# A hybrid encoder layer on one core: GpSimd's readers of SBUF go to VectorE or ScalarE, and the planner's dense matmul gets another cost

## The chip, the cores and the metric

The kernel runs on one core of a Trainium2 chip. The core has five engines with a queue of instructions each: TensorE (PE, matmuls from SBUF into PSUM), VectorE (DVE), ScalarE (ACT), GpSimd (POOL) and SyncE (SP), which here issues nearly all transfers. Each engine works through its queue in order, and an instruction waits until the results that it reads are there. The metric is the time of one execution in microseconds (us), as the median of several runs.

## The reference

One layer of a streaming encoder is applied to 2048 prompt frames and 32 frames of a running stream, 2080 columns in all, 1024 features wide, in float32. After an RMS norm, one input projection feeds three groups of mixers that read the frames in time order: an RG-LRU (256 features), an RWKV-7 (6 heads of 64, a state of 64 x 64 a head) and an mLSTM (6 heads of 64). Their outputs go through one output projection; a SwiGLU network with 2816 hidden units follows, and a last RMS norm.

```python
hn = rmsnorm(x, norm1)
proj = hn @ w_in                                    # 1024 x 3072
ya = rmsnorm(rg_lru(...), norm_a) * gelu(pa_g)      # columns one after another
yb = rwkv7_mix(...); yc = mlstm_mix(...)
x = x + concat([ya, yb, yc]) @ w_out                # 1024 x 1024
gu = rmsnorm(x, norm2) @ w_ffn_in                   # 1024 x 5632
x = x + (silu(gu[:, :2816]) * gu[:, 2816:]) @ w_ffn_out
y = rmsnorm(x, norm_f)                              # and all new states
```

## The kernel before

**Stages.** The columns are cut into four parts: three of 512 and one of 544 (512 prompt and 32 sample columns, worked as two blocks of 272). Every projection holds features on the partitions and columns along the free dimension. `innorm` and `inproj` do the norm and the input projection of a part, 24 row tiles of 128 outputs, and write them to a scratch in DRAM (`spill`). `mixers` reads that back in pieces of 128 columns, 16 for the prompt and a last one of 32 sample columns: 17 groups of an RWKV, an mLSTM and an RG-LRU part each, which write `ymix` in DRAM. `phase2` does output projection, SwiGLU and the sums for a part; it needs that part's `ymix`. All four input projections come first, then mixers and `phase2` of each part in turn.

**Dense matmuls.** A projection is made of three float32r products: every weight block and every activation is split into a leading part and the exact rest (`split`: ScalarE copies the leading part, another engine subtracts). `mm3` adds leading x leading, leading x rest and rest x leading into one PSUM tile `pj`. In the names `wh`/`wl` are the two parts of a weight block of 128x1024, `hh`/`hl` those of hidden units, or of a weight block in the hidden units' place, `ah`/`al` those of the normed input. In `inproj`, GpSimd makes the weights' rests (`load_w(..., G, True)`); elsewhere VectorE does.

**A group of the RWKV.** Decays and removal keys are normed (`k<-k,k` are Newton steps of the key norm's inverse root, 128x6), the bonus is summed by a product with `bones` (its operand split into `ch` and `cl`), and products `rw<-Fr,BK` give the chunk's interaction matrices `Hr`. Their 32-blocks are inverted row by row on VectorE (`utmp` and `Z`, 62 instructions in line, after and before a trip through DRAM). `rw<-ta,Hr` and `rw<-c,En` complete the inverse; then come the state products (`SV`, `zc`, `UV`, `Un`), the head norm (`yx`) and the write to `ymix`.

**Who sets the order.** Nothing is emitted while the program is written down. A `Recorder` notes each instruction with its operands and a level of urgency (`EVAC`, `WGT`, `NORM`, `MIX`, `PROJ`, `LATE`); `Recorder.order` then fills the engines' queues by list scheduling: the engine that can start first takes its most urgent instruction that is ready, by the durations that `cost` states. So a cost changes no instruction, only places in the queues. On TensorE the mixers' products have a share: each adds its planned time to `debt`, each projection matmul takes `RATE` = 0.45 of its own planned time off, and mixers are held back while `debt` is too high or too few are ready.

```python
if eng == "dve":
    if name in ("tensor_copy", "tensor_scalar") and ins[0].space != PSUM:
        return 68.0 + 0.53 * n, 127.0
...
    return 68.0 + 1.04 * n + (61.0 if ptr and n > 1 and len(ins) > 1 else 0.0), 127.0
...
return 125.0 + (2.15 if name == "tensor_tensor" else 1.0) * n, 127.0      # GpSimd
```

All instructions are emitted from one line (L332 of the profile), so the profile tells them apart by their tiles.

Of the kernel before, what the change touches and what calls it, by code (L numbers as in the profile page):

```python
# [11 lines left out]
F32 = mybir.dt.float32  # L12
F32R = mybir.dt.float32r
I32 = mybir.dt.int32
AF = mybir.ActivationFunctionType
# [12 lines left out]
# columns of the per-feature vectors, 128 features a column  # L28
# [13 lines left out]
# columns of the constants  # L42
# [11 lines left out]
# columns of the small weights  # L54
# [41 lines left out]
class Cfg:  # L96
    def __init__(self, seq, sb1, sb2):
        # sb1: list of (prompt tokens, column blocks); the 32 sample tokens follow the last prompt token
        # sb2: list of (first column, column blocks)
        self.seq = seq  # L100
        self.T = seq + 32
        self.sb1 = sb1
        self.sb2 = sb2
# [10 lines left out]
# PE's share for the mixers, relative to the projections, and how long they may hold it at a time (ns)  # L114
RATE = 0.45
BURST = 1200.0
# allowance for the mixers' operands (ns)
# [13 lines left out]
# transfers issued ahead of the one under way (ns)  # L131
WINDOW = 3000.0
# the projection's tile before which the next columns are normed
NEXT = 14
# urgency, on the other engines and on PE; the lowest goes first
# [12 lines left out]
class Recorder:  # L148
    """Stands in for the engines: notes each instruction with its operands, so that the order of issue
    can be chosen before the instructions are emitted (under tc.manual_schedule, which keeps it)."""  # L150
# [93 lines left out]
    def order(self):  # L244
        """greedy: the engine that can start first takes its most urgent instruction that is ready"""
# [102 lines left out]
def cost(eng, name, out, ins, kw):  # L348
    """nanoseconds on the engine, and until another engine sees the result"""
# [8 lines left out]
    if eng == "pe":  # L358
# [3 lines left out]
        if st.dtype == F32R:  # L362
            return max(n, 256) / 2.4 + 2.7, 196.0
# [26 lines left out]
class Tiles:  # L390
    """fixed tiles, taken in turn: name -> bufs tiles"""
# [30 lines left out]
def hybrid_kernel(ctx, tc, A, O, cfg):  # L422
# [48 lines left out]
    def rsqrt_(x, y, t, it=3):  # L471
        """y = 1/sqrt(x), Newton from the exponent halved"""
# [7 lines left out]
    def log1p_(e, out2, tmp):  # L480
        """out2 = log(1+e)/2 for 0 <= e <= 1, by the series of atanh(e/(2+e)); tmp: two tiles"""
# [10 lines left out]
    # the gates' weights, row selections; histories and running states: stream 0 the prompt, 1 the sample  # L492
# [11 lines left out]
    def setup():  # L504
# [9 lines left out]
        # derived vectors  # L514
# [8 lines left out]
        # -4 softplus(-lam)  # L523
# [1114 lines left out]
```

## Time and profile before

| | |
|---|---|
| runs | 2943.65, 2947.76 and 2950.33 us, median 2947.76 us |
| span of the profiled execution, first to last instruction | 2943.6 us (its whole time is not given) |
| instructions | 48657 |
| mean granted clock of TensorE | 0.979 of full speed |
| dense matmuls | 7056 of 512 columns, 4704 of 272 |
| HBM | 268.51 MB read, 46.27 MB written, 107 GB/s over the span |

The page lists for each engine the time in which it was busy. That is an average over stretches that differ: at first input projections and mixers run together, then `phase2` of the first three parts with the mixers, and in the last part `phase2` alone. A table by stretches keeps them apart. The granted clock is a mean over a stretch: 1.00 is 2.4 GHz, and 0.5 would be 1.2 GHz throughout. Names are the program's tiles, output first (`wl<-raw,wh`), buffer numbers left out; sizes are partitions x elements.

### The profile page before, as it was taken

The numbers are of one execution on the slowest core, as the hardware profiler recorded it, in microseconds if no ns is written. First come the engines' busy times: TensorE is split into PE (matmuls) and PEld (weight loads), VectorE is DVE, ScalarE is ACT, GpSimd is POOL, SyncE is SP. The second block draws the span as 40 slices with busy tenths as digits, with TensorE's granted clock in tenths as the row PEclk, the third lists the DMA queues.
The fourth block names the chain that finished last, engine by engine and source line by source line (L and its number), as shares of the span: only waits on it lengthen the run. The fifth ranks groups of instructions, "written<-read, shape, count | busy, mean of one in ns | idle before, by whom it ended". The sixth has DMA issues, their size and how long they took to land.

```text
span 2943.6 us, 48657 instructions
## 1 busy us (share of the span) xinstructions
PE 2797.9 (95%) x17643; PEld 2301.3 (78%) x17643; DVE 2190.3 (74%) x5580; ACT 1217.7 (41%) x2555; POOL 704.9 (24%) x839
## 2 busy tenths in 40 slices
PE   7989889989999999999999999999999999999998
PEld 6767667778877777777777777777777778999998
DVE  6776887777778877888888887888666776555555
ACT  4444454444454434445544444363433334322223
POOL 5644344344312011112311011122011112211102
PEclk9999999999999999999999999999999999999999
DMA  6353334253433233324433323334332334232222
GB/s 210 112 160 109 123 123 128 100 165 100 122 100 98 82 104 99 91 72 128 139 111 92 96 87 101 93 107 138 93 107 82 93 87 162 74 90 87 87 90 81
DMA packets 235212, 317.95 MB, mean 108 GB/s; under 512 B 63100, under 2 KB 146988, under 8 KB 234844
## 3 DMA queue, kind: packets, MB, share of 16 engines
q1 hardware_dynamic: 233820, 313.74, 35.0%
q8 instruction: 138, 2.26, 0.3%
q10 hardware_dynamic: 1152, 1.11, 0.1%
q14 instruction: 102, 0.84, 0.1%
HBM read 268.51 MB, written 46.27 MB: 107 GB/s over the span
## 4 chain that ended last, share of the span: by engine, by line
PE 61%; DVE 20%; DMA 5%; issue 2%; ACT 2%; POOL 1%; SPq 0%; DVEq 0%; ACTq 0%; POOLq 0%
PE pj L332 51%; PE rw L332 7%; DVE wl L332 4%; PE ml L332 3%; DMA xs<-tb 3%; DVE utmp L332 1%; DVE Z L332 1%; DVE stg L332 1%; DVE x L332 1%; DVE k L332 1%; DMA tb<-Hr 1%; DVE Fr L332 1%; DVE R L332 1%; DVE al L332 1%; DVE Dm L332 1%
## 5 line engine op out<-in xcount | busy, mean ns | idle before, releaser
L332 PE MATMUL pj<-ah,wh 128*128 128x512 f32 (+1 forms) x2560 | 905.8, 361 | 4.1 <-ACT cbuf L332 1.8
L332 PE MATMUL pj<-al,wh 128*128 128x512 f32 (+1 forms) x2560 | 903.8, 360 | 4.4 <-DVE al L332 4.4
L332 PE MATMUL pj<-ah,wl 128*128 128x512 f32 (+1 forms) x2560 | 836.4, 358 | 2.0 <-DVE wl L332 2.0
L332 ACT ACTIVATE wh<-raw 128x1024 fp32r<-128x1024 f32 (+2 forms) x444 | 382.2, 862 | 759.2 <-PE pj L332 587.5
L332 PEld LDWEIGHTS pj<-ah,wh 128*128 128x128 f32 x2560 | 488.6, 191 | 73.1 <-issue 2.7
L332 PEld LDWEIGHTS pj<-al,wh 128*128 128x128 f32 x2560 | 490.7, 192 | 69.2 <-DVE al L332 6.0
L332 PEld LDWEIGHTS pj<-ah,wl 128*128 128x128 f32 x2560 | 458.8, 191 | 71.4 <-DVE wl L332 3.0
L332 DVE TENSOR_TENSOR wl<-raw,wh 128x1024 fp32r<-128x1024 f32 (+2 forms) x397 | 412.6, 1041 | 61.7 <-ACT wh L332 58.7
L332 POOL TENSOR_TENSOR stg<-stg,rb 128x512 f32<-128x512 f32 (+1 forms) x110 | 155.2, 1419 | 893.8 <-DVE stg L332 771.0
L332 PE MATMUL pj<-hl,wh 128*128 128x512 f32 (+1 forms) x856 | 302.2, 360 | 2.7 <-DVE hl L332 2.1
L332 PE MATMUL pj<-hh,wh 128*128 128x512 f32 (+1 forms) x856 | 299.7, 361 | 3.5 <-ACT hh L332 3.5
L332 PE MATMUL pj<-hh,wl 128*128 128x512 f32 (+1 forms) x856 | 279.5, 356 | 0.0
L332 DVE TENSOR_TENSOR x<-x,pj 128x512 f32<-128x512 f32 (+1 forms) x280 | 159.1, 583 | 134.9 <-PE pj L332 133.2
L332 PEld LDWEIGHTS pj<-hl,wh 128*128 128x128 f32 x856 | 161.6, 189 | 28.3 <-DVE hl L332 7.0
L332 PEld LDWEIGHTS pj<-hh,wh 128*128 128x128 f32 x856 | 160.1, 188 | 28.8 <-ACT hh L332 6.7
L332 PE MATMUL pj<-ah,hh 128*128 128x512 f32 (+1 forms) x480 | 173.1, 367 | 7.3 <-ACT hh L332 5.8
L332 PE MATMUL pj<-al,hh 128*128 128x512 f32 (+1 forms) x480 | 174.7, 370 | 2.5 <-DVE al L332 2.5
L332 DVE TENSOR_TENSOR utmp<-Z,xs 96x60 f32<-96x60 f32 (+27 forms) x527 | 135.7, 258 | 51.1 <-DMA xs<-tb 36.4
L332 PEld LDWEIGHTS pj<-hh,wl 128*128 128x128 f32 x856 | 152.3, 188 | 22.3
L332 POOL TENSOR_TENSOR wl<-raw,wh 128x1024 fp32r<-128x1024 f32 x47 | 114.8, 2444 | 191.1 <-ACT wh L332 186.9
L332 PE MATMUL pj<-ah,hl 128*128 128x512 f32 (+1 forms) x480 | 160.1, 365 | 0.0
L332 POOL TENSOR_TENSOR hl<-raw,hh 128x512 fp32r<-128x512 f32 x92 | 126.7, 1379 | 114.6 <-ACT hh L332 106.1
(348 smaller groups left out, 4222.1 us busy)
## 6 DMA issues: line engine op xcount, KB each, us to landing
raw<-in_w_ffn_in SPq DMA_DIRECT2D x176, 512.0 KB
raw<-in_w_ffn_out SPq DMA_DIRECT2D x128, 256.0 KB
raw<-in_w_in SPq DMA_DIRECT2D x96, 256.0 KB
raw<-in_w_in SPq DMA_DIRECT2D x48, 512.0 KB
spill<-stg SPq DMA_DIRECT2D x72, 256.0 KB
raw<-in_w_out SPq DMA_DIRECT2D x32, 512.0 KB
x<-in_xT SPq DMA_DIRECT2D x48, 256.0 KB
raw<-in_w_ffn_out SPq DMA_DIRECT2D x64, 192.0 KB
```

What stands on the lines that cost most here:

```text
L332: o.fn(*o.args, **o.kw)
```

## The change

Every GpSimd instruction that reads SBUF goes to another engine: two-operand arithmetic and the scalings to VectorE, copies to ScalarE. GpSimd keeps memsets. In the planner the matmul with float32r operands costs n / 2.25 + 4.0 ns instead of n / 2.4 + 2.7. Comments and docstrings are removed as well, which touches no instruction.

```diff
 # the planner's cost of a matmul with float32r operands (n: columns): ns on the engine, ns to the reader
-            return max(n, 256) / 2.4 + 2.7, 196.0
+            return max(n, 256) / 2.25 + 4.0, 196.0
 # innorm, square(k)
-                G.tensor_tensor(out=acc, in0=acc, in1=sq, op=ALU.add)
+                V.tensor_tensor(out=acc, in0=acc, in1=sq, op=ALU.add)
 # inproj, conv()
-                G.tensor_copy(buf[:, 0:3], hist[st])
-                G.tensor_copy(hist[st], buf[:, m:m + 3])
+                S.activation(buf[:, 0:3], hist[st], AF.Copy)
+                S.activation(hist[st], buf[:, m:m + 3], AF.Copy)
 # inproj
-            w = first_w.pop(0) if first_w else load_w(w_in(m), 8, G, True)
+            w = first_w.pop(0) if first_w else load_w(w_in(m), 8, V, True)
-                        G.tensor_copy(tm[:, 0:1], histmu[st][:, m:m + 1])
-                        G.tensor_copy(histmu[st][:, m:m + 1], tm[:, q:q + 1])
+                        S.activation(tm[:, 0:1], histmu[st][:, m:m + 1], AF.Copy)
+                        S.activation(histmu[st][:, m:m + 1], tm[:, q:q + 1], AF.Copy)
 # rglru: four instructions, G to V
-            G.tensor_scalar(out=la[:, m, :], in0=tr[:, m, :], scalar1=1.0, scalar2=D("nsp", i=m),
+            V.tensor_scalar(out=la[:, m, :], in0=tr[:, m, :], scalar1=1.0, scalar2=D("nsp", i=m),
...
-        G.tensor_tensor(out=q, in0=q, in1=gb, op=ALU.mult)
+        V.tensor_tensor(out=q, in0=q, in1=gb, op=ALU.mult)
 # rwkv
-        G.tensor_tensor(out=cl_, in0=cf, in1=ch_.bitcast(F32), op=ALU.subtract)
+        V.tensor_tensor(out=cl_, in0=cf, in1=ch_.bitcast(F32), op=ALU.subtract)
-            G.tensor_copy(UV[oh, :, :nch, j, :], SVt[oh, :, :nch, j, :])
+            S.activation(UV[oh, :, :nch, j, :], SVt[oh, :, :nch, j, :], AF.Copy)
-                G.tensor_copy(UN[c][hs, :, j, :], UV[hs, :, c, j, :])
+                S.activation(UN[c][hs, :, j, :], UV[hs, :, c, j, :], AF.Copy)
 # phase2
-                G.tensor_tensor(out=acc[:, o:o + N], in0=acc[:, o:o + N], in1=sq, op=ALU.add)
+                V.tensor_tensor(out=acc[:, o:o + N], in0=acc[:, o:o + N], in1=sq, op=ALU.add)
-                    G.tensor_tensor(out=u, in0=u, in1=rb2[:, o:o + N], op=ALU.mult)
+                    V.tensor_tensor(out=u, in0=u, in1=rb2[:, o:o + N], op=ALU.mult)
-                        (G if last and k % 3 == 2 else V).tensor_tensor(out=y, in0=y, in1=rb, op=ALU.mult)
+                        V.tensor_tensor(out=y, in0=y, in1=rb, op=ALU.mult)
```

The order of issue follows from the new engines and the new cost. VectorE's queue, in the first group's key norm (`k_0_230`, `k_0_233` and `k_0_236` are its three small tiles; `ca`, `stg` and `sq<-pj` belong to the input projection, `BK` and `c` to the group), read before:

```order
L332 TENSOR_SCALAR k_0_233<-k_0_230 128x6
L332 SCALAR_TENSOR_TENSOR stg_202<-stg_202,ca_206 128x512
L332 TENSOR_TENSOR sq_180<-pj_199,acc_126 128x512
L332 TENSOR_TENSOR k_0_236<-k_0_233 128x6
L332 TENSOR_TENSOR BK_240<-sq_228,En_226 64x6x64
L332 SCALAR_TENSOR_TENSOR k_0_236<-k_0_236,k_0_230 128x6
L332 TENSOR_TENSOR BK_240<-sq_228,En_226 64x6x64
L332 SCALAR_TENSOR_TENSOR k_0_233<-k_0_236,k_0_233 128x6
L332 TENSOR_TENSOR k_0_236<-k_0_233 128x6
L332 SCALAR_TENSOR_TENSOR k_0_236<-k_0_236,k_0_230 128x6
L332 SCALAR_TENSOR_TENSOR k_0_233<-k_0_236,k_0_233 128x6
```

and in the changed kernel:

```order
L332 TENSOR_SCALAR k_0_233<-k_0_230 128x6
L332 TENSOR_TENSOR BK_240<-sq_228,En_226 64x6x64
L332 SCALAR_TENSOR_TENSOR stg_202<-stg_202,ca_206 128x512
L332 TENSOR_TENSOR sq_180<-pj_199,acc_126 128x512
L332 TENSOR_TENSOR wl_144<-raw_141,wh_142 128x1024
L332 TENSOR_TENSOR k_0_236<-k_0_233 128x6
L332 TENSOR_TENSOR c_168<-c_168,sq_228 128x384
L332 SCALAR_TENSOR_TENSOR k_0_236<-k_0_236,k_0_230 128x6
L332 SCALAR_TENSOR_TENSOR ca_206<-cbuf_205,vec_76,ca_206 128x512
L332 TENSOR_TENSOR hl_0_147<-raw_140,hh_0_146 128x512
L332 SCALAR_TENSOR_TENSOR ca_206<-cbuf_205,vec_76,ca_206 128x512
L332 TENSOR_TENSOR acc_127<-acc_127,sq_180 128x512
```

The weights' rests (`wl`, `hl`) and the row sums (`acc`) of the next columns now stand between the steps of the key norm.

TensorE's queue at the last RWKV group, where its inverse is completed and its state used (`pj` are dense matmuls, here of the third `phase2`, `rw` the group's), read before:

```order
L332 MATMUL pj_201<-al_0_171,wh_142 128x512
L332 MATMUL rw_165<-ta_167,Hr_125 32x32 x6
L332 MATMUL pj_201<-ah_0_170,wl_144 128x512
L332 MATMUL pj_201<-ah_0_172,wh_142 128x512
L332 MATMUL pj_201<-al_0_173,wh_142 128x512
L332 MATMUL pj_201<-ah_0_172,wl_144 128x512
L332 MATMUL rw_166<-c_168,En_226 32x32 x6
L332 MATMUL rw_165<-SV_150,Fr_124 64x64 x4
L332 MATMUL pj_201<-ah_0_174,wh_142 128x512
L332 MATMUL pj_201<-al_0_175,wh_142 128x512
```

and in the changed kernel, where the dense matmuls are already those of the last `phase2` (272 columns):

```order
L332 MATMUL pj_200<-ah_0_172,wh_143 128x272
L332 MATMUL pj_200<-al_0_173,wh_143 128x272
L332 MATMUL pj_200<-ah_0_172,wl_145 128x272
L332 MATMUL rw_165<-ta_167,Hr_125 32x32 x6
L332 MATMUL rw_166<-c_168,En_226 32x32 x3
L332 MATMUL rw_165<-SV_150,Fr_124 64x64
L332 MATMUL rw_166<-c_168,En_226 32x32 x3
L332 MATMUL rw_165<-SV_150,Fr_124 64x64 x3
L332 MATMUL rw_166<-zc_229,c_168 64x64 x6
L332 MATMUL rw_165<-UV_247,Fr_124 64x64 x6
L332 MATMUL rw_166<-Un_0_120,Hr_125 64x128
```

The group's products follow each other now with no dense matmul between them; before, dense matmuls stood between most of the steps.

## Rows read from the trace of the kernel before

**Rows 1.** page, part 1: busy us (share of the span) xinstructions

```profile
PE 2797.9 (95%) x17643; PEld 2301.3 (78%) x17643; DVE 2190.3 (74%) x5580; ACT 1217.7 (41%) x2555; POOL 704.9 (24%) x839
```

**Rows 2.** busy by stretch: stretch, us, five engines, TensorE's clock, DMA share, GB/s

```profile
0.00:120.30 120.30, 98.86 (x432) 76.94 (x432) 78.75 (x126) 55.46 (x99) 70.08 (x85) 0.98 0.53 177
120.30:846.50 726.20, 662.48 (x4462) 544.09 (x4463) 554.45 (x1527) 335.83 (x775) 298.65 (x389) 0.96 0.40 124
846.50:2430.30 1583.80, 1543.60 (x8959) 1198.50 (x8957) 1280.88 (x3416) 660.85 (x1395) 245.58 (x287) 0.99 0.34 100
2484.00:2943.60 459.60, 443.20 (x3493) 440.20 (x3491) 239.19 (x442) 138.59 (x238) 77.44 (x69) 0.98 0.30 90
```

**Rows 3.** TensorE's waits, 120.3 to 846.5: us in total, times, longest

```profile
PE rw L332 <- ACT ch L332: 9.9, 3, 6.1
PE ml L332 <- DVE gt L332: 8.1, 2, 5.4
```

**Rows 4.** chain that ended last, in order of time: start, us, what

```profile
2035.35 40.85 PE pj L332 x175
2796.82 125.52 PE pj L332 x997
```

**Rows 5.** timeline at 109 to 121: start, us, engine, line, operation, [idle before]

```profile
109.31 2.40 POOL L332 TENSOR_TENSOR wl<-raw,wh 128x1024 fp32r<-128x1024 f32 x1 [2.24 <-ACT wh L332]
109.52 2.21 DVE L332 TENSOR_TENSOR k<-k 128x6 f32<-128x6 f32 x1
120.31 0.69 PE L332 MATMUL rw<-ch,bones 128*128 128x384 f32 x1 [6.13 <-ACT ch L332]
```

**Rows 6.** VectorE's groups by shape: xcount | busy us, mean ns | idle before

```profile
L332 DVE TENSOR_TENSOR wl<-raw,wh 128x1024 fp32r<-128x1024 f32 x209 | 289.2, 1384 | 21.9 <-ACT wh L332 20.8
L332 DVE TENSOR_TENSOR x<-x,pj 128x512 f32<-128x512 f32 x168 | 114.2, 683 | 60.1 <-PE pj L332 58.5 <-DMA x<-in_xT 0.2
L332 DVE TENSOR_TENSOR x<-x,pj 128x272 f32<-128x272 f32 x112 | 44.9, 434 | 74.9 <-PE pj L332 74.7
L332 DVE TENSOR_TENSOR hl<-stg,hh 128x272 fp32r<-128x272 f32 x44 | 30.5, 694 | 4.8 <-ACT hh L332 4.8
L332 DVE SCALAR_TENSOR_TENSOR k<-k,k 128x6 f32<-128x6 f32 x96 | 34.7, 361 | 0.9
```

**Rows 7.** VectorE's instructions of two tiles: xcount: ns min/median/max

```profile
L332 DVE SCALAR_TENSOR_TENSOR k<-k,k x102: 145/166/2190, 112.1 to 2366.0; 128x6 f32<-128x6 f32 x96, 64x6 f32<-64x6 f32 x6
L332 DVE TENSOR_TENSOR utmp<-Z,xs x527: 135/209/2457, 159.0 to 2421.9; 96x60 f32<-96x60 f32 x16, 96x28 f32<-96x28 f32 x12, 96x66 f32<-96x66 f32 x11, 96x48 f32<-96x48 f32 x10
```

**Rows 8.** page, part 5: a group, xcount | busy us, mean ns | idle before

```profile
L332 DVE TENSOR_TENSOR utmp<-Z,xs 96x60 f32<-96x60 f32 (+27 forms) x527 | 135.7, 258 | 51.1 <-DMA xs<-tb 36.4
```

**Rows 9.** GpSimd's groups by shape

```profile
L332 POOL TENSOR_TENSOR wl<-raw,wh 128x1024 fp32r<-128x1024 f32 x47 | 114.8, 2444 | 191.1 <-ACT wh L332 186.9 <-PE ml L332 4.1
L332 POOL TENSOR_TENSOR hl<-raw,hh 128x512 fp32r<-128x512 f32 x92 | 126.7, 1379 | 114.6 <-ACT hh L332 106.1 <-PE rw L332 2.6 <-ACT En L332 2.3
L332 POOL TENSOR_TENSOR stg<-stg,rb 128x512 f32<-128x512 f32 x66 | 105.1, 1593 | 558.3 <-DVE stg L332 435.5 <-DVE utmp L332 69.7 <-DVE Z L332 46.5
L332 POOL TENSOR_TENSOR stg<-stg,rb 128x272 f32<-128x272 f32 x44 | 50.0, 1157 | 335.6 <-DVE stg L332 335.6
L332 POOL TENSOR_TENSOR acc<-acc,cbuf 128x512 f32<-128x512 f32 x42 | 70.6, 1680 | 117.3 <-ACT cbuf L332 117.0
L332 POOL TENSOR_TENSOR acc<-acc,sq 128x512 f32<-128x512 f32 x21 | 31.4, 1497 | 12.7 <-ACT ah L332 6.3 <-DVE sq L332 5.4 <-ACT sq L332 0.4
```

**Rows 10.** ScalarE's copy of 64x192, by shape

```profile
L332 ACT ACTIVATE SV<-rw 64x192 f32<-64x192 f32 x66 | 21.4, 325 | 12.5 <-PE rw L332 11.6
```

**Rows 11.** timeline at the last RWKV group's end

```profile
2430.30 0.38 PE L332 MATMUL rw<-ta,Hr 32*32 32x32 f32 x12
2452.41 0.40 PE L332 MATMUL rw<-cst,yx 64*128 64x64 f32 x3
2466.45 1.75 DVE L332 TENSOR_TENSOR al<-sq,ah 128x544 fp32r<-128x544 f32 x2 [0.60 <-ACT ah L332]
```

More of the change, by code (lines that the diff above doesn't have):

```diff
@@ L855, in rglru @@
         S.activation(s2, h, AF.Square)
-        G.tensor_tensor(out=s2[:, 0, :], in0=s2[:, 0, :], in1=s2[:, 1, :], op=ALU.add)
+        V.tensor_tensor(out=s2[:, 0, :], in0=s2[:, 0, :], in1=s2[:, 1, :], op=ALU.add)
         rb = la[:, 0, :]
@@ L863, in rglru @@
         S.activation(q, gb, AF.Square)
-        G.tensor_scalar(out=q, in0=q, scalar1=0.044715, scalar2=1.0, op0=ALU.mult, op1=ALU.add)
-        G.tensor_tensor(out=q, in0=q, in1=gb, op=ALU.mult)
+        V.tensor_scalar(out=q, in0=q, scalar1=0.044715, scalar2=1.0, op0=ALU.mult, op1=ALU.add)
+        V.tensor_tensor(out=q, in0=q, in1=gb, op=ALU.mult)
         S.activation(q, q, AF.Tanh, scale=math.sqrt(2.0 / math.pi))
```

## The prediction

> **What bounds the kernel now.** I read the page's busy line first. TensorE is busy 2797.9 of 2943.6 us, VectorE 2190.3, ScalarE 1217.7, GpSimd 704.9 [rows 1]. TensorE's work is the same in both kernels, so the question is what TensorE loses: idle time, and time at the lower clock. The table by stretches shows it [rows 2]. Up to 120.3 us TensorE is idle for 120.30 - 98.86 = 21.4 us. From 120.3 to 846.5 us (the input projections, with the first five groups of mixers beside them) it is idle for 63.7 us, and the granted clock is 0.96; with only two levels, 1.2 and 2.4 GHz, that is 8% of the stretch at the lower one, where half the time is lost: 0.04 x 726.2 = 29 us. Together 93 us, about 18.6 us a group. From 846.5 to 2430.3 us it loses 40.2 us idle and 0.01 x 1583.8 = 16 us of clock, 56 us over eleven groups, 5 us each. After 2484 it loses some 26 us, mostly in the last few microseconds.
>
> Then the list of waits for the second stretch: TensorE waits there for ScalarE's and VectorE's operands of the mixers, not of the projections [rows 3]. In the chain a dense matmul of 512 columns takes 40.85 / 175 = 233.4 ns and one of 272 columns 125.52 / 997 = 125.9 ns [rows 4].
>
> Last, why operands come late. In the timeline a VectorE multiplication of 128x6, a step of the key norm, takes 2.21 us; it starts 0.21 us into a GpSimd subtraction of 2.40 us and ends with it. At 120.31 TensorE has idled 6.13 us [rows 5]. The shapes confirm it: with one operand in PSUM, 272 columns take 434 ns on VectorE, with both in SBUF 694; `k<-k,k` has a median of 166 ns and a mean of 361 [rows 6, 7]. VectorE waits while GpSimd reads SBUF, and the planner counts none of it.
>
> **The change part by part.**
>
> *GpSimd's work becomes VectorE's.* The prices are those of rows with a PSUM operand: 683 ns at 512 columns, 434 at 272, so 1.04 ns a column, and 683 + 512 x 1.04 = 1214 ns at 1024 [rows 6]. Then [rows 9]: 47 `wl` x 1.214 = 57; 92 `hl` x 0.683 = 63; 66 and 44 `stg` = 45 + 19; 42 `acc<-acc,cbuf` = 29; 21 `acc<-acc,sq` = 14; together 227 us, for 499 us of GpSimd's 705. The other 206 us are GpSimd's memsets (which stay), copies and small arithmetic; at most a third of that is new VectorE work. I take 260 us in all.
>
> *What VectorE gets back* has no row of its own. From below: 209 `wl` x (1384 - 1214) = 36; 96 `k` steps x (361 - 166) = 19; 44 `hl` x (694 - 434) = 11; 527 `utmp` x (258 - 209) = 26 [rows 6 to 8]; that is 92 us in four groups out of some 370. From above: all GpSimd time, 705 us. I take 250, since the four groups hold under a quarter of VectorE's time and the many unlisted two-operand groups show the same inflated means. VectorE then ends at 2190 + 260 - 250 = 2200 us, as busy as before; at the floor it would be 2358, or 80%.
>
> The Trainium skill's page "SBUF — State Buffer", section "Who interferes with whom", says that a VectorE instruction with two SBUF inputs contends with a GpSimd instruction that reads SBUF, and not with one that only writes it. By that rule the memsets left behind cost nothing and every such wait is returned, however small its group; the rows bear out the first half (694 against 434), and the third rival below is what it would be worth.
>
> *GpSimd's copies become ScalarE's.* Those are 192 tiny ones, 34 `UV<-SV` and 66 `Un<-UV`. At most 0.325 us each for all but the 34 [rows 10] and twice that for those: under 106 us on an engine that is idle 59% of the span. I cost it at nothing; if the 66 `Un` copies were late, TensorE would wait about 0.7 us in each of 33 chunks, 23 us.
>
> *The planner's matmul* goes from 216.0 to 231.6 ns at 512 columns, where 233.4 was measured, and from 116.0 to 124.9 at 272, where it was 125.9. VectorE's planned 600 ns at 512 columns stays under the measured 683. So before, the plan took TensorE for 8% and VectorE for 14% too fast, with the waits on GpSimd on top; now 1% and 14%, with none. In the first stretch VectorE's whole lag behind TensorE shrinks; in the middle one, where GpSimd is busy 16% of the time against 41% [rows 2], little changes.
>
> *What the order makes of it.* In TensorE's queue 371 dense matmuls of 512 columns stand before the first group's `bones` product in the old order and 363 in the new; before the sixth group's, 1774 of 512 and 1152 of 272 columns, against 2018 and 1152. So TensorE has 252 more matmuls, 252 x 0.2334 = 59 us, to fill the first five groups' waits. In the first group, 5 dense matmuls stand between the `bones` product and the spread of the key norm, now 41. The mixers' own VectorE work takes as long as before, so these 59 us come out of the 93 lost. I take 60, since that leaves 33 us or 6.6 a group, near the middle stretch's 5 [rows 2]. Bounds: 30 (a third of the loss) and 85. The first 120 us: VectorE takes the row sums as well, but works without GpSimd beside it; -3, bounds +6 and -8. Middle stretch: 0, bounds +15 and -28 (half its loss). Last stretch: 0.
>
> *The bill at the end.* The mixers then run later against the projections: at the last group's `bones` product 6861 matmuls of 512 columns have been issued instead of 6672. In the old order 118 dense matmuls of the third `phase2`, 27.5 us, still stand behind the last group's `ta,Hr`, between its remaining steps. In the new one none is left: the whole rest of the last RWKV group stands in TensorE's queue with nothing between, and behind it the output projection's third row tile, which reads that group's result. In the trace this chain runs from 2430.30 to the `al` tiles that end at 2468.2 us, 38 us, and hides behind matmuls [rows 11]. Alone it should be somewhat shorter, since TensorE's queue no longer delays its steps: 32 us, bounds 22 and 38. Less about 3 us of TensorE's own work in it, plus 2 for the lower clock after it, in proportion to the first stretch's 29 us on 64 of idling, of which such a long single stop should need less. And the 32-block inverse before it has 153 matmuls of 512 columns and 24 of 272 as cover, 39 us, instead of 212 of 512, 49 us: 0 to 11 us short, I take 4. Together +35, bounds +22 and +50. Nowhere else does the new order put so many of the mixers' steps in a row.
>
> **Sum.** 2943.6 - 60 - 3 + 35 = 2915.6 us for the span. The timed median, 2947.76, stands 4.2 us above the profiled span; the page has no other time of that execution, so I carry the difference: **2920 us**.
>
> **Rivals.**
>
> *VectorE becomes the bound (slower).* If it gets back only the floor, in the first stretch it has 554 + 120 of the new work - 38 (its 42% of 92) = 636 us in 726, 88%, where the middle stretch runs with 81% [rows 2]. The 48 us above that share come off the 60: 2943.6 - 12 - 3 + 35 + 4 = 2968. It decides once VectorE passes some 85% before 846 us. For it: `wl`, the row sums and the key norm now share one in-order queue. Against: the contended rows. The Trainium skill's "Perfetto Trace Analysis", section "Optimizing Scalar/DVE Operations", advises giving work to ScalarE or even GpSimd where VectorE is saturated, and adds that between VectorE and GpSimd it might not help because they share a port; the first half is this rival, the second the forecast.
>
> *What is saved early is paid back at the end (no change).* The mixers alone set when the last `phase2` can start, and 189 matmuls x 0.2334 = 44 us gained early are 44 us waited at the end: 2943.6 - 45 - 3 + 45 + 4 = 2945. For it: the order's positions. Against: TensorE, at 97% busy, bounds the middle stretch, so time saved early should move the mixers too.
>
> *The waits on GpSimd were most of the loss (faster).* Then the first stretch gives 80, the middle half of its 56, and the end chain costs 32: 2943.6 - 80 - 28 - 3 + 32 + 4 = 2869. For it: 2.21 us for a step of 0.17 [rows 5, 7]. Against: VectorE's 14% stays, and the weights' remainders now stand among the key norm's steps.
>
> **How the numbers follow.** Forecast 0.47, with its own range 2895 to 2941; faster rival 0.20; no change 0.14; slower 0.19. Cutting the outer half of the two outer rivals leaves 2869 to 2968 for 8 in 10. No change means within 0.2% (5.9 us), about what this kernel's measurement can tell: faster 0.67, same 0.14, slower 0.19.
>
> **What would show it.** `k<-k,k` of 128x6 with a mean near 166 ns and `hl` of 272 columns near 434; VectorE busy near 2200 us; TensorE's idle time plus clock loss from the start to the sixth group's `bones` down to about 55 us; one stop of 25 us or more before the last `phase2`, at `rw<-ta,Hr` to `pj<-ah`. I am wrong if that stop is absent, if VectorE is above 2300 us, or if the first stretch still loses over 70 us.

## The result, and the profile after

The changed kernel takes 2873.81 us (median of 4 runs, 2866.23 to 2877.09), the one before 2946.62 us beside it: ratio 0.9741, 95% interval 0.9727 to 0.9756, so 2.6% faster. The forecast was 2920. The direction came as forecast, and so did the sizes in the first stretch (first to sixth `bones` product) and at the stop at the end; the gain everywhere else was put at 3 us and was 45 us.

Busy time of the engines, from the page (its first line is the span), against [rows 1]:

```profile
span 2874.6 us, 48278 instructions
...
PE 2776.3 (97%) x17643; PEld 2292.2 (80%) x17643; DVE 2151.0 (75%) x6026; ACT 1282.0 (45%) x2847; POOL 15.9 (1%) x101
```

VectorE has 446 more instructions and is busy 39 us less. The stretches, cut at the first `bones` product, the sixth and the last; then the stop, and the rest of the last `phase2` (the 49 us from the last `bones` to the stop, without idle time, are left out). Columns are those of [rows 2], whose third row runs on to the last `ta,Hr`; up to the last `bones` the kernel before has this row:

```profile
846.50:2363.60 1517.10, 1477.12 (x8667) 1146.55 (x8666) 1231.12 (x3297) 641.70 (x1366) 238.56 (x281) 0.99 0.34 100
```

and the changed kernel has these:

```profile
0.00:104.10 104.10, 96.51 (x425) 77.30 (x426) 70.13 (x151) 60.48 (x129) 2.16 (x19) 0.98 0.61 202
104.10:832.90 728.80, 709.64 (x4793) 583.51 (x4792) 587.70 (x1802) 395.23 (x1009) 5.03 (x30) 0.98 0.42 131
832.90:2314.30 1481.40, 1454.64 (x8535) 1130.39 (x8533) 1189.06 (x3394) 651.91 (x1408) 8.51 (x51) 0.99 0.34 102
2363.40:2417.00 53.60, 22.35 (x152) 19.71 (x151) 23.46 (x76) 11.17 (x23) 0.00 (x0) 0.55 0.41 135
2417.00:2874.60 457.60, 444.09 (x3526) 442.55 (x3524) 241.32 (x513) 139.13 (x238) 0.00 (x0) 0.99 0.28 86
```

In the second row TensorE idles 728.80 - 709.64 = 19 us, where it idled 64, and does 331 more matmuls in nearly the same time. In the fourth it is busy 22 of 54 us at a granted clock of 0.55, nearly all at 1.2 GHz, after idling: that is the stop at the end.

What TensorE loses (idle time, and half of its busy time at the lower clock), summed over the trace (sums differ from the span by rounding). The first three rows are called head, first stretch and middle below:

```
stretch                              before   after   change   forecast
start to the first bones               22.9     9.3    -13.6      -3
first to sixth bones                   90.5    32.1    -58.4     -60
sixth to last (17th) bones             56.4    39.9    -16.5       0
last bones to start of last phase2      0.6     0.0     -0.6       -
its first 60 matmuls: the stop          5.1    40.2    +35.1     +35
rest of the last phase2                 7.2     1.1     -6.1       0
tail                                   13.6    13.5     -0.1       0
TensorE's own busy time, full clock  2747.1  2738.7     -8.4       0
span                                 2943.6  2874.6    -69.0     -28
```

VectorE's long waits are gone. The timeline at the first group of mixers, against [rows 5]:

```profile
99.96 1.22 DVE L332 TENSOR_TENSOR wl<-raw,wh 128x1024 fp32r<-128x1024 f32 x1
...
101.09 0.16 DVE L332 TENSOR_TENSOR k<-k 128x6 f32<-128x6 f32 x1
...
104.07 0.34 PE L332 MATMUL rw<-ch,bones 128*128 128x384 f32 x1
```

The weights' remainder takes VectorE 1.22 us where GpSimd took 2.40, the step of the key norm 0.16 us instead of 2.21, and the `bones` product comes 16 us earlier, without idle time ahead of it. VectorE's groups by shape (count, busy us, mean ns) and the minimum, median and maximum of two tiles, against [rows 6, 7]:

```profile
L332 DVE TENSOR_TENSOR wl<-raw,wh 128x1024 fp32r<-128x1024 f32 x256 | 312.2, 1220 | 30.8 <-ACT wh L332 25.5 <-PE rw L332 2.9 <-PE pj L332 0.8
L332 DVE TENSOR_TENSOR x<-x,pj 128x512 f32<-128x512 f32 x168 | 114.4, 682 | 57.0 <-PE pj L332 53.0 <-DMA x<-in_xT 2.4
L332 DVE TENSOR_TENSOR hl<-stg,hh 128x272 fp32r<-128x272 f32 x44 | 18.8, 437 | 5.9 <-ACT hh L332 5.0
L332 DVE SCALAR_TENSOR_TENSOR k<-k,k 128x6 f32<-128x6 f32 x96 | 15.1, 158 | 0.9
```
```profile
L332 DVE SCALAR_TENSOR_TENSOR k<-k,k x102: 128/157/170, 101.6 to 2314.7; 128x6 f32<-128x6 f32 x96, 64x6 f32<-64x6 f32 x6
L332 DVE TENSOR_TENSOR utmp<-Z,xs x527: 99/207/235, 151.5 to 2377.4; 96x60 f32<-96x60 f32 x16, 96x28 f32<-96x28 f32 x12, 96x66 f32<-96x66 f32 x11, 96x48 f32<-96x48 f32 x10
```

The means now lie at the medians: the `hl` of 272 columns went from 694 to 437 ns, `k<-k,k` from 361 to 158, and the maxima of over 2.1 us are gone. With a PSUM operand (`x<-x,pj`) nothing changed, 683 to 682.

TensorE's waits in the first stretch (in total, times, longest), against [rows 3]: ScalarE's `ch`, whose 9.9 us stood first, is no longer among the long ones.

```profile
PE ml L332 <- DMA xi<-spill: 4.6, 2, 3.8
PE ml L332 <- DVE wl L332: 2.4, 1, 2.4
PE ml L332 <- DVE gt L332: 2.0, 2, 1.7
```

The stop at the end, TensorE's timeline with the idle time and its releaser in brackets, against [rows 11]:

```profile
2373.54 0.43 PE L332 MATMUL pj<-ah,wl 128*128 128x272 f32 x1
2388.54 0.26 PE L332 MATMUL rw<-ta,Hr 32*32 32x32 f32 x2 [14.57 <-DVE ta L332]
...
2402.23 0.58 PE L332 MATMUL rw<-cst,yx 64*128 64x64 f32 x3 [5.33 <-DVE yx L332]
2410.01 1.28 PE L332 MATMUL pj<-ah,wh 128*128 128x272 f32 x4 [7.21 <-ACT ah L332]
```

Last, a row of both kernels that the prediction should have read. VectorE's timeline, first before, then after:

```profile
1145.46 0.69 DVE L332 TENSOR_TENSOR x<-x,pj 128x512 f32<-128x512 f32 x1
1146.06 0.69 DVE L332 TENSOR_TENSOR wl<-raw,wh 128x512 fp32r<-128x512 f32 x1
1146.66 0.68 DVE L332 TENSOR_TENSOR x<-x,pj 128x512 f32<-128x512 f32 x1
1147.26 0.69 DVE L332 TENSOR_TENSOR wl<-raw,wh 128x512 fp32r<-128x512 f32 x1
```
```profile
955.71 0.68 DVE L332 TENSOR_TENSOR stg<-stg,pj 128x512 f32<-128x512 f32 x1
956.31 0.68 DVE L332 TENSOR_TENSOR wl<-raw,wh 128x512 fp32r<-128x512 f32 x1
956.91 0.68 DVE L332 TENSOR_TENSOR stg<-stg,rb 128x512 f32<-128x512 f32 x1
```

Each is recorded with 0.68 to 0.69 us, and the next starts 0.60 us after it. So 600 ns, which the planner takes, is what such an instruction holds VectorE for; 683 is what the record shows.

### The profile page after: what moved, and what is told of

Same layout as the page of the kernel before. It is cut to its first block, busy times and chain, and to the rows that moved or that the text cites. A ratio compares the mean times of both kernels' runs of the same rounds, so it can differ in the third digit from the quotient of the medians.

```text
span 2874.6 us, 48278 instructions
## 1 busy us (share of the span) xinstructions
PE 2776.3 (97%) x17643; PEld 2292.2 (80%) x17643; DVE 2151.0 (75%) x6026; ACT 1282.0 (45%) x2847; POOL 15.9 (1%) x101
## 4 chain that ended last, share of the span: by engine, by line
PE 74%; DVE 13%; DMA 7%; ACT 3%; issue 2%; SPq 1%; DVEq 0%; ACTq 0%
PE pj L332 62%; PE rw L332 8%; PE ml L332 4%; DVE wl L332 3%; DMA xs<-tb 3%; DVE stg L332 1%; DVE Z L332 1%; DVE utmp L332 1%; DMA c<-zb 1%; DMA tb<-Hr 1%; DVE x L332 1%; DMA sq<-ymix 1%; DMA zb<-Z 1%; DVE hl L332 1%; SPq L332 1%
## 5 line engine op out<-in xcount | busy, mean ns | idle before, releaser
L332 PE MATMUL pj<-ah,wh 128*128 128x512 f32 (+1 forms) x2560 | 897.3, 358 | 10.9 <-ACT ah L332 8.6
L332 PE MATMUL pj<-al,wh 128*128 128x512 f32 (+1 forms) x2560 | 898.8, 358 | 0.4 <-DVE al L332 0.4
L332 PE MATMUL pj<-ah,wl 128*128 128x512 f32 (+1 forms) x2560 | 832.4, 357 | 0.5 <-DVE wl L332 0.5
L332 ACT ACTIVATE wh<-raw 128x1024 fp32r<-128x1024 f32 (+2 forms) x444 | 382.5, 862 | 706.4 <-PE pj L332 565.7
L332 PEld LDWEIGHTS pj<-ah,wh 128*128 128x128 f32 x2560 | 483.2, 189 | 78.2 <-ACT ah L332 10.1
L332 PEld LDWEIGHTS pj<-al,wh 128*128 128x128 f32 x2560 | 485.3, 190 | 63.6 <-issue 0.8
L332 PEld LDWEIGHTS pj<-ah,wl 128*128 128x128 f32 x2560 | 454.3, 189 | 68.2 <-issue 1.8
L332 DVE TENSOR_TENSOR wl<-raw,wh 128x1024 fp32r<-128x1024 f32 (+2 forms) x444 | 432.6, 975 | 64.1 <-ACT wh L332 58.1
L332 PE MATMUL pj<-hh,wh 128*128 128x512 f32 (+1 forms) x856 | 301.9, 363 | 7.8 <-ACT hh L332 7.8
L332 PE MATMUL pj<-hl,wh 128*128 128x512 f32 (+1 forms) x856 | 302.6, 361 | 0.0
L332 PE MATMUL pj<-hh,wl 128*128 128x512 f32 (+1 forms) x856 | 281.6, 359 | 0.0
L332 DVE TENSOR_TENSOR x<-x,pj 128x512 f32<-128x512 f32 (+1 forms) x280 | 158.9, 582 | 129.3 <-PE pj L332 124.8
L332 PEld LDWEIGHTS pj<-hh,wh 128*128 128x128 f32 x856 | 162.3, 190 | 33.5 <-ACT hh L332 10.0
L332 PEld LDWEIGHTS pj<-hl,wh 128*128 128x128 f32 x856 | 163.3, 191 | 22.7 <-DVE hl L332 0.8
L332 PE MATMUL pj<-ah,hh 128*128 128x512 f32 (+1 forms) x480 | 171.7, 364 | 7.1 <-ACT hh L332 5.8
L332 PE MATMUL pj<-al,hh 128*128 128x512 f32 (+1 forms) x480 | 171.9, 364 | 0.7 <-DVE al L332 0.7
L332 PEld LDWEIGHTS pj<-hh,wl 128*128 128x128 f32 x856 | 153.8, 190 | 23.3 <-issue 0.4
L332 PE MATMUL pj<-ah,hl 128*128 128x512 f32 (+1 forms) x480 | 157.0, 359 | 0.0
L332 DVE TENSOR_TENSOR utmp<-Z,xs 96x60 f32<-96x60 f32 (+27 forms) x527 | 107.2, 203 | 59.5 <-DMA xs<-tb 50.8
L332 DVE TENSOR_TENSOR stg<-stg,pj 128x512 f32<-128x512 f32 (+1 forms) x110 | 62.3, 582 | 81.9 <-PE pj L332 81.1
L332 DVE TENSOR_TENSOR cbuf<-pj,acc 128x512 f32<-128x512 f32 (+1 forms) x110 | 62.7, 586 | 71.7 <-PE pj L332 69.1
L332 DVE TENSOR_TENSOR Z<-Z,utmp 96x60 f32<-96x60 f32 (+27 forms) x527 | 107.1, 203 | 7.0
```

The costliest lines, as they stand in the source:

```text
L332: o.fn(*o.args, **o.kw)
```

## The experiments

Theory W: VectorE's waits while GpSimd reads SBUF made the mixers' operands late in every stretch, and the planner's VectorE cost was right. Rivals: C, the dearer matmul and the order it makes brought the gain; V, the prediction's premise, the plan takes VectorE 14% too fast. Theories K and L are on the stop at the end: K, dense matmuls issued early are missing behind the last group, so a larger share for the mixers removes the stop; L, the last group's chain sets the end in any order. Theory B, against W in e8, is that any GpSimd work, or tiles held longer, costs the time.

**The planner's cost alone** (e1: before with it):

```
-            return max(n, 256) / 2.4 + 2.7, 196.0
+            return max(n, 256) / 2.25 + 4.0, 196.0
```

> Before with the planner's new matmul cost alone; GpSimd keeps all its reading work. In the order the mixers then stand earlier against the projections: before the sixth group's bones product 1728 matmuls of 512 columns and 921 of 272, where before had 1774 and 1152, and the last group's ta,Hr has some 620 matmuls of 512 columns behind it. Theory W (waits on GpSimd, in every stretch, made VectorE late; its recorded 683 ns at 512 columns overlap the next instruction by some 80 ns, so the planned 600 were right): less cover, waits untouched, so first stretch to the sixth bones loses as much as before or more (95 to 130 us, was 112 from the start), middle stretch 50 to 65, no stop at the end: 2940 to 2990 us. Theory C (the planner's dearer matmul gave the middle and head gains): losses in the middle fall to 35 or so and the first 100 us lose under 10: 2905 or less.

Measured 3035.48 us, ratio 1.0291 [1.0266, 1.0317]: slower, and by more than either theory had. First and second stretch:

```profile
0.00:118.10 118.10, 101.91 (x420) 78.44 (x421) 73.71 (x118) 55.34 (x99) 65.76 (x81) 0.95 0.53 177
118.10:836.10 718.00, 644.75 (x4197) 522.45 (x4198) 535.62 (x1505) 322.53 (x745) 296.66 (x378) 0.93 0.38 118
```

TensorE loses 21 us up to the first `bones`, 120 to the sixth, 112 in the middle. The middle's 112 are about twice what W had there. The cost brings the mixers forward while their operands are as late as before. C falls as a cause by itself.

**The moves alone** (e2: after with the old cost, the same line the other way round):

> After with the old matmul cost: GpSimd's reads are moved, the planner still takes 216.0 ns for 512 columns. In the order the mixers stand later still: the last group's bones product comes behind all 7056 matmuls of 512 columns. Theory W: losses before the last group as in after (about 7 us in the first 105 us, 30 to the sixth bones, 40 in the middle) and a longer stop at the end, 60 to 110 us in place of 35: 2895 to 2950 us, with VectorE's steps as short as in after (k<-k,k mean near 166 ns). Theory C: the middle and first losses return to 56 and 21 us, and the stop at the end comes on top: over 2930 us.

Measured 2972.56 us, ratio 1.0076 [1.0055, 1.0097]: slower than before, though no wait on GpSimd is left and the first two stretches lose least of all kernels (6 and 24 us). That is 23 us over W's range; the total is one that C allowed. Stretches three and four, and TensorE's long waits in the fourth:

```profile
877.80:2400.00 1522.20, 1456.42 (x8372) 1140.14 (x8372) 1186.78 (x3375) 649.39 (x1384) 8.86 (x52) 0.96 0.33 98
2400.00:2504.00 104.00, 34.84 (x297) 28.72 (x298) 43.61 (x165) 20.68 (x64) 0.45 (x3) 0.53 0.19 61
```
```profile
2416.51 0.85 PE L332 MATMUL rw<-ta,Hr 32*32 32x32 f32 x24 [14.86 <-DVE ta L332]
2438.80 0.90 PE L332 MATMUL rw<-cst,yx 128*128 128x128 f32 x3 [4.02 <-DVE yx L332]
2481.81 0.53 PE L332 MATMUL rw<-ta,Hr 32*32 32x32 f32 x12 [23.03 <-DVE ta L332]
```

The stop is there twice, for the 16th group and for the last. And theory W's 40 us for the middle were wrong: idle time alone is 66 us there, because the same stop comes ahead of the second and third `phase2` as well. A table by group shows it: a group's cover, which is the dense matmuls between its `bones` product and the next one's, in us at 0.2334 and 0.1259 us each [rows 4], and what TensorE loses in the same time.

```
group            1      2      3      4      5      6      7      8      9     10     11     12     13     14     15     16
before      104/21  96/23  94/17  90/15  88/15 107/7  106/8   95/8  112/4  105/7  101/2  102/3  105/8  109/7  102/1   98/2
after       134/8  111/8   97/3   93/6   98/8   97/6   99/2  104/6  130/5   92/4  102/1   95/5  121/7   97/1   99/2   95/0
e1 cost      88/25  93/25  91/22  84/25  80/23  96/9   92/6   98/12  99/9  110/15  95/11 100/8   95/13 104/13  98/11  89/4
e2 moves    137/1  112/2  122/2   94/10 123/9  109/3  113/2   70/36 132/8  108/1  110/1   65/40 143/8  107/0  109/1   56/44
share 0.53  119/6  113/6  106/8   86/6  102/5   95/2   94/5   92/2  123/10  95/3   99/6   92/4  105/8  102/2   98/7   91/1
```

In e2 the groups 8 and 12, each the last of its part, and 16, the last of the prompt, have 56 to 70 us of cover and lose 36 to 44: the next `phase2` can't start without their part's result, and the dense matmuls of the one before are used up. What was issued early is missing there. In the middle's other eight groups e2 loses 25 us where before lost 43, so the losses that C expected back don't come back; neither theory had the stops.

**Only the input projections' reads moved** (e3: before with the new cost, and the edits below, all four history copies alike):

```
-                G.tensor_tensor(out=acc, in0=acc, in1=sq, op=ALU.add)
+                V.tensor_tensor(out=acc, in0=acc, in1=sq, op=ALU.add)
...
-                G.tensor_copy(hist[st], buf[:, m:m + 3])
+                S.activation(hist[st], buf[:, m:m + 3], AF.Copy)
...
-            w = first_w.pop(0) if first_w else load_w(w_in(m), 8, G, True)
+            w = first_w.pop(0) if first_w else load_w(w_in(m), 8, V, True)
```

> Before with the new cost, and only the input projections' GpSimd reads moved (weights' remainders and their low parts, row sums, the histories' copies); the mixers and the third phase keep theirs. In the order the sixth bones comes behind 2020 and 1152 matmuls, the last ta,Hr at 6792 of 7056, so no stop at the end. Theory W: head and first stretch lose as little as after (7 and 30 to 40 us) since GpSimd's reads there are gone, middle and last stretches lose about what before lost (50 to 60 and 8), no stop of 35 us: 2875 to 2900 us. Theory C: middle loses 40 or less although phase2's GpSimd reads are still there: 2860 or less.

Measured 2915.2 us, ratio 0.9876 [0.9849, 0.9903], 15 us over the expected range. Head and first stretch lose 9 and 38 us, nearly as after, there is no stop, the middle loses 87 where W had 50 to 60, and the rest of the last `phase2` 17 where W had 8:

```profile
103.60:842.20 738.60, 710.43 (x4808) 583.59 (x4807) 596.99 (x1785) 392.00 (x990) 58.10 (x105) 0.99 0.43 130
842.20:2305.60 1463.40, 1401.04 (x8227) 1079.92 (x8227) 1163.94 (x3165) 609.00 (x1309) 236.21 (x271) 0.98 0.34 98
```

GpSimd's 236 us in the second row are what the full change also moves. With 96.5 us of cover a group the eleven middle groups lose 7.9 us each; the kernel with the share at 0.53 below has 98.7 us, no reads, and loses 4.5. So the reads of `phase2` and of the mixers are worth up to 3.4 us a group, 37 us; the 2 us less of cover are in that.

**GpSimd reads again, in after's order** (e6), the waits without the move: one added read behind each weight's rest of the input projections, each row sum (`innorm` and `phase2`) and each hidden unit. The queues of TensorE, VectorE and ScalarE are those of after, row for row; the tiles that are read are also held longer, which e8 below shares:

```
-        o.dur, o.lat = cost(eng, name, out, ins, kw)
+        o.dur, o.lat = (0.0, 0.0) if eng == "pool" and name == "tensor_tensor" else cost(eng, name, out, ins, kw)
...
+                G.tensor_tensor(out=r, in0=r, in1=wh.bitcast(F32), op=ALU.subtract)
...
+                G.tensor_tensor(out=sq, in0=sq, in1=sq, op=ALU.add)
...
+                    G.tensor_tensor(out=u, in0=u, in1=rb2[:, o:o + N], op=ALU.mult)
```

> After, with the same order of issue, and GpSimd instructions added beside VectorE's: one that reads SBUF behind each weight remainder, row sum and hidden unit of the projections, in place on tiles that nothing reads any more, planned at no time. It measures the port waits alone. Theory W: VectorE's two-operand rows swell again (k<-k,k mean over 300 ns), losses return in head, first and middle stretches, half to all of the 14 + 58 + 23 + 8 us gained there: 2915 to 2975 us. Theory C (order and planner's cost made the gain, GpSimd beside VectorE matters little): within 12 us of after, 2862 to 2886 us.

Measured 3063.15 us, ratio 1.0384 [1.0364, 1.0405]: 190 us over after, beyond what W had; C falls. The mean of `k<-k,k` rose from 158 to 228 ns, where W had over 300. Here VectorE has the moved work and the waits, so the loss is larger than before's. Its timeline at the first group, then the busy line:

```profile
117.45 2.73 POOL L332 TENSOR_TENSOR raw<-raw,wh 128x1024 f32<-128x1024 f32 x1 [4.82 <-DVE k L332]
...
117.83 2.37 DVE L332 SCALAR_TENSOR_TENSOR k<-k,k 128x6 f32<-128x6 f32 x1
```
```profile
PE 2829.6 (92%) x17643; PEld 2319.9 (76%) x17643; DVE 2377.8 (78%) x6026; ACT 1287.5 (42%) x2847; POOL 511.2 (17%) x441
```

The 2.2 us step of [rows 5] is back beside a new neighbour. The same 6026 VectorE instructions take 2377.8 - 2151.0 = 227 us longer. Losses: head 24 us (after 9), first stretch 157 (32), middle 63 (40); the first two stretches:

```profile
0.00:119.40 119.40, 102.94 (x425) 81.02 (x425) 95.60 (x147) 59.83 (x128) 57.63 (x50) 0.93 0.52 172
119.40:976.60 857.20, 749.30 (x4791) 609.23 (x4792) 721.42 (x1804) 398.52 (x1011) 255.53 (x175) 0.93 0.37 112
```

**Reads in `phase2` alone** (e9: of these lines those on `sq` and `u` in `phase2`):

> After, in the same order, with GpSimd reading again only beside phase2's hidden units and row sums (in place, results unused, planned at no time). Theory W (the middle and last stretches gained because these reads are gone): first stretches as in after, the middle loses 55 to 70 us instead of 40, the last stretch 3 to 8 instead of 1: 2885 to 2915 us. Theory C (the middle gained by where the mixers stand): 2866 to 2882.

Measured 2917.49 us, ratio 0.988 [0.9858, 0.9902], against 2868.72 and 0.9717 [0.9702, 0.9733] for after on the same chip; 2 us over W's range and far outside C's. The stretches:

```profile
101.00:826.50 725.50, 704.32 (x4792) 579.19 (x4791) 590.50 (x1800) 395.57 (x1010) 14.91 (x38) 0.99 0.43 132
826.50:2344.50 1518.00, 1464.26 (x8533) 1131.17 (x8532) 1243.83 (x3396) 652.89 (x1408) 131.25 (x141) 0.99 0.34 99
```

The first stretch is after's (27 us lost; 32 and 27 in the two profiles of after). The middle takes 1518.0 us, where after took 1481.4 and 1479.1, and loses 69 us instead of 40 and 36. That is the term that the prediction had at 0. Nothing uses the added results, so it isn't GpSimd's own slow steps (in before, TensorE's idle time that ends with a GpSimd result is only 4.4 us in the first stretch and 6.1 in the middle); and it isn't that the tiles are held longer, since e8 below, which holds them too, loses 37 us in the middle.

**GpSimd nearly as active, but only writing** (e8: two memsets of the same tile in place of each added instruction of e6):

> As the kernel in which GpSimd reads SBUF again, but each added instruction is two memsets of the same tile, which only write: GpSimd is about as busy. Theory W (it is GpSimd's reading that VectorE waits for): within 20 us of after, 2860 to 2895 us, k<-k,k and hl means as in after. Theory B (any GpSimd work, or the weights' tiles held longer, costs the time): 2990 to 3080 us.

Measured 2903.49 us, ratio 0.9852 [0.9835, 0.9868], 8 us over W's range, 160 under e6. First stretch, busy line, then one of its waits in the timeline (L333 is L332 of the others):

```profile
103.60:854.00 750.40, 713.01 (x4792) 584.24 (x4793) 594.49 (x1801) 396.05 (x1011) 189.01 (x318) 0.98 0.42 128
```
```profile
PE 2771.2 (96%) x17643; PEld 2285.9 (79%) x17643; DVE 2160.7 (75%) x6026; ACT 1283.0 (44%) x2847; POOL 389.5 (13%) x781
```
```profile
113.27 0.95 POOL L333 MEMSET raw<- 128x1024 f32 x1 [0.87 <-DVE wl L333]
...
113.32 0.93 DVE L333 TENSOR_SCALAR rsypj<-rsxpj 128x4 int32<-128x4 int32 x1
113.40 0.85 DVE L333 SCALAR_TENSOR_TENSOR k<-k,k 128x6 f32<-128x6 f32 x1
```

Here 390 us of GpSimd cost VectorE 10 us, where e6's 511 cost 227. B falls as the main cause: 160 of e6's 190 us are the reading. Some 30 are not. The profiled execution, the shortest of the four, has a span 17 us longer than after's, and the first stretch alone has 18 us more idle time of TensorE; VectorE's 10 us don't hold all of it, and the rest is open (the weights' tiles are held longer, which was not tried by itself).

**The planner's VectorE cost times 1.14** (e4: after, with):

```
-            return 68.0 + 0.53 * n, 127.0
+            return 1.14 * (68.0 + 0.53 * n), 127.0
...
-        return 68.0 + 1.04 * n + (61.0 if ptr and n > 1 and len(ins) > 1 else 0.0), 127.0
+        return 1.14 * (68.0 + 1.04 * n + (61.0 if ptr and n > 1 and len(ins) > 1 else 0.0)), 127.0
```

> After with the planner's VectorE costs times 1.14 (683 ns at 512 columns, as recorded, in place of 600). In the order the mixers stand later: 2260 and 1152 matmuls before the sixth bones, all 7056 of 512 columns before the last group's. Theory W (600 was right, VectorE's recorded time overlaps the next instruction): no fewer waits in the middle, and the last group without cover as in the kernel with the old matmul cost: 2940 to 2990 us. Theory V (the prediction's premise: the plan took VectorE 14% too fast, and that makes operands late): the middle stretch from the sixth to the last group's bones loses under 25 us instead of 40, the stop at the end 60 to 110 instead of 35 us: 2880 to 2930.

Measured 3037.68 us, ratio 1.0297 [1.0279, 1.0316]: V is refuted, and W's range missed by 48 us at its upper end. Groups 8, 12 and 16 have 70, 31 and 42 us of cover and lose 43, 61 and 46. With 683 ns in the planner the last group of each part comes later, to where the cover is used up; that 600 ns is right is read from the starts above, not from this run.

**The mixers' share** (after with one number; 0.53 and 0.55 in the same way, and after itself once more):

```
-RATE = 0.45
+RATE = 0.50
```

> After with the planner's share for the mixers at 0.50 instead of 0.45. In the order the mixers stand earlier: 2010 and 1152 matmuls before the sixth bones, 6626 before the last group's, and 182 matmuls of 512 columns still stand behind its ta,Hr. Theory K (cover is conserved: dense matmuls spent early are missing at the last group): the 35 us stop at the end is gone, eleven middle groups with 98 us of cover each instead of 103 lose 40 to 60 us: 2835 to 2865 us. Theory L (the last group's chain sets the end whatever the order): a stop of 25 us or more remains, 2865 to 2885.

> After with the share at 0.55: 1951 and 1152 matmuls before the sixth bones, 6759 before the last group's, 67 of 512 columns behind its ta,Hr (16 us). Theory K: the stop at the end shrinks to 5 to 20 us, the stretches before lose about 5 to 15 us more than in after: 2845 to 2880 us. Theory L: stop of 25 us or more, 2870 to 2900.

> After once more, beside the kernel with the share at 0.50 on the same chip: 2866 to 2882 us, ratio to before 0.972 to 0.977.

> The share at 0.50 once more, beside after. Theory K (the stop at the end is bought off with cover from the middle): 5 to 15 us under after. If the first difference of 10 us was the chips' spread: within 4 us of after.

> The share at 0.53: the order that comes nearest to that of 0.50 at the end (6648 matmuls of 512 columns before the last group's bones, 170 behind its ta,Hr), 1995 and 1152 before the sixth bones. Theory K: no stop at the end, the middle loses 45 to 60 us: 2855 to 2872 us. If the share itself matters and not the places: over 2875.

```
share                us      ratio to before            stop   middle   rest of last phase2
0.45 (after)      2873.81   0.9741 [0.9727, 0.9756]     40.2     39.9       1.1
0.45 again        2868.72   0.9717 [0.9702, 0.9733]     40.3     36.2       1.1
0.50              2863.84   0.9711 [0.9693, 0.9729]      0.0     49.8       9.2
0.50 again        2859.18   0.9688 [0.9672, 0.9704]      0.0     48.7       9.1
0.53              2850.38   0.9651 [0.9633, 0.9668]      0.0     49.4       8.7
0.55              2880.77   0.9770 [0.9755, 0.9784]     11.5     49.6       2.6
```

(the last three columns: us that TensorE loses). K holds at 0.50 and 0.53, where the stop is gone for about 10 us more in the middle and 8 behind; 0.50 came out at the upper edge of its first range and, beside after, 9.5 us under it, inside its second; 0.53 came out 5 us under its own, and after itself at 0.9717, just under its expected ratio. L falls. At 0.55 the stop shrinks to 11.5 us, as K has it, but the stretches before it lose 18 us more than in after, where K had 5 to 15, and the total is just over its range. The share works through where the last groups come to stand, not monotonically: behind the last group's `bones`, 0.55 leaves 69 us of matmuls of 512 columns, 0.50 and 0.53 leave 100 and 95. The kernel at 0.53 beats after on the same chip by 2868.72 - 2850.38 = 18 us, 0.6%, and before by 3.5%; its last group of mixers and the rest of the run:

```profile
2271.40:2383.40 112.00, 112.00 (x586) 90.49 (x585) 84.40 (x199) 48.53 (x85) 0.13 (x1) 1.00 0.35 105
2383.40:2848.80 465.40, 445.91 (x3526) 444.23 (x3525) 245.55 (x520) 138.19 (x237) 0.00 (x0) 0.98 0.31 94
```

In the first row TensorE doesn't idle at all, where after stops for 31 us.

## Why the prediction was right or wrong

*What bounds the kernel.* Right: TensorE, and its losses to operands made late by VectorE's waits. None of the signs of being wrong came, and the loss up to the sixth `bones` went to 41 us, below the 55 expected.

*What VectorE gets back (250).* Right, somewhat low. The 47 `wl`, 221 instructions of 512 columns and 44 of 272 that it took over cost 47 x 1.13 + 221 x 0.60 + 44 x 0.35 = 201 us from start to start, and yet it is busy 39 us less: at least 240 us came back, and more with the small ones. The forecast of 2200 us for its busy time was 49 high; 26 of it is new work priced by recorded durations, at 227 us for these. That "every such wait is returned", which the prediction weighed with its third rival, holds: summed over VectorE's records that exceed the median of the same instruction in after by over 60 ns, the excess falls from 276 us to 0.2. The Trainium skill's page "SBUF — State Buffer", section "Who interferes with whom", whose rule on GpSimd's reads the prediction weighed, is borne out by e6 against e8 (227 us and 10).

*First stretch (-60).* The size is right, -58, and the reason mostly isn't. The prediction let 252 more matmuls fill the same waits. At equal cover the waits themselves are smaller: groups 2 to 5 of before, with 88 to 96 us of cover, lose 17 us each, groups 3 to 5 of after, with 93 to 98, lose 5. Twelve us in each of five groups are 60 without any help from cover, and groups 1 and 2, which got the most of it, lose 8 each, no less than the others. In e6 the same order with the waits put back loses 157.

*Head (-3), middle (0).* Here the forecast failed, by 27 us together, with 8 of TensorE's own time and 6 of the last `phase2` besides, which it had at nothing. The head's 13.6 us lie outside its bound of 8, the middle's 16.5 inside its bound of 28. The step was that "VectorE's planned 600 ns at 512 columns stays under the measured 683 ... in the middle one ... little changes." The 683 ns overlap the next instruction by 80; the plan was right on VectorE but for the waits, and with these gone and the matmul's cost corrected it is within about 1% on both at these sizes. So the gain is wherever GpSimd read: 13.6 us in the head, where the prediction set the row sums' move against the waits, and e3, which of the reads moves just those of the input projections, has it all (it loses 9.1 us there, e1 with the cost alone 20.7); 16.5 in the middle, where e9 takes 29 to 33 us back. The Trainium skill's page "Perfetto Trace Analysis", in the section that the prediction cited ("Optimizing Scalar/DVE Operations"), says in brackets that a profiled latency has about twice the fixed overhead, since its second half overlaps the next instruction. The trace agrees: 683 - 512 x 1.04 = 150 ns recorded and, with 602 ns as the median from start to start, 602 - 532 = 70 held.

*The bill at the end (+35).* Right in place and reason, `rw<-ta,Hr` to `pj<-ah`; that the size, +35.1, agrees so well is luck, since three terms were off and nearly cancel. The wait for the 32-block inverse was taken at 4 us, at most 11, and was 14.6. The chain behind it was taken at 32 us, 22 to 38, and took 2410.01 - 2388.54 = 21.5, with 13.8 of them idle. The lower clock was taken at 2 us, less than in proportion to the idling, and cost 40.2 - 31.3 = 8.9. What the bill hid was the rest of the last `phase2`: its -6 is not a gain of the moves, since 0.50 and 0.53, without the stop, lose 9 there, about before's 7. That the stop lets the leftovers of the mixers finish fits this, but was not tried by itself.

*The new matmul cost.* The prediction read it as a correction that shifts cover. It is more: without it the moves are slower than before (1.0076), and without the moves it is (1.0291). The table by group shows the two working against each other: the moved work, which the planner counts on VectorE, delays the mixers, and the dearer matmul calls them back before each `phase2`.

*The rivals.* VectorE as the bound: its busy share in the first stretch is 587.70 / 728.80 = 81%, and the losses fell. No change: the sixth and the last `bones` come 13.6 and 49 us earlier, and the end takes 35 back. The faster rival, 2869, was the one that came: its mechanism in all stretches, with -80 and -28 where -58 and -16.5 were measured. That its total is so near is luck in part: 33 us too much there stand against 25 in the head, the last `phase2` and TensorE's own time that it lacked.

What stays open: by what TensorE's own busy time fell 8.4 us for the same matmuls, and the rest of e8's loss. The former goes with GpSimd's reads: in after's very order it is 2738.7 and 2739.7 us in the two profiles of after, 2748.4 in e9 and 2750.6 in e6, and 2742.3 in e8.

## What to carry to other kernels

Before a planned time is called wrong by a profile, read the intervals between starts of back-to-back instructions, not the recorded durations. Where a plan ignores a wait, the loss can show in every stretch in which the two engines meet, as it did here, so price its removal by stretch from the stretch's own inflated rows, not by what the order adds as cover. The dense matmuls are a fixed stock: those issued early are missing at the next point where everything waits for the last group, and that point is worth a look at the share of work before anything else.

## What the runs showed of the hardware

A one-input VectorE instruction can wait for a memset. In e8, of 56 `TENSOR_SCALAR` with their input in SBUF that overlap a memset by over 0.1 us, 36 were recorded over 60 ns above the median of the same instruction in after, and of 711 with two inputs in SBUF 14; 13 of these 14 stand behind a one-input instruction that waits and end with it. Beside GpSimd's two-input reads in before, counted in the same way, 285 of 440 instructions with two inputs in SBUF were, and none of 127 `TENSOR_TENSOR` with an operand in PSUM. The Trainium skill's page "SBUF — State Buffer", in its section "Who interferes with whom", has both: `tensor_scalar` can enter a mode that takes the shared ports, two inputs contend with reads alone.
